# Expert tokens fetched by indirect DMA and transposed, instead of gathered by one-hot matmuls, in a trunk layer on one Trainium2 core

## The chip, the cores and the metric

The kernel runs on one core of a Trainium2 chip. The metric is the device time of one execution in microseconds. Engines: PE (TensorE: matmuls; PEld its weight loads), DVE (VectorE), ACT (ScalarE), POOL (GpSimd), SP (SyncE, which issues nearly all DMAs here).

## The reference, cut to what matters

A hybrid decoder layer on 512 tokens of 1024 features: a token mixer (RWKV-7 and sparse attention), a layer norm, then a mixture of 32 SwiGLU experts (top-1 of 4 groups, top-2 of 8 experts inside it), and a second layer norm. Everything is float32. The change is in the second half:

```
D_MODEL, SEQ, N_EXPERTS, TOP_K_INNER, D_EXPERT = 1024, 512, 32, 2, 512

def _hier_moe(x, wg, bg, we, be, w1, w3, w2):
    g_prob = jax.nn.softmax((xf @ wg + bg), axis=-1)
    grp = jnp.argmax(g_prob, axis=-1)
    ...
    top_v, top_i = lax.top_k(e_logits, TOP_K_INNER)      # inside the group
    top_w = jax.nn.softmax(top_v, axis=-1) * p_grp[:, None]
    ...
    xs = xpad[row_tok].reshape(n_blk, MOE_BLOCK, D)      # tokens of each expert
    def expert_block(args):
        xb, e = args
        h = jax.nn.silu(xb @ w1[e]) * (xb @ w3[e])
        return h @ w2[e]
    ys = lax.map(expert_block, (xs, blk_exp)).reshape(n_rows, D)
    out = jnp.zeros((N + 1, D), f32).at[row_tok].add(ys * row_w[:, None])

x = _layer_norm(ALPHA * x + token_mixer(x), ln1_g, ln1_b)
x = _layer_norm(ALPHA * x + _hier_moe(x, ...), ln2_g, ln2_b)
```

## The kernel before, in words

Up to about 560 us the mixer runs; then comes the output projection of its last columns with the first layer norm and the router (to 606 us), and then the experts. Instructions are recorded engine by engine and a tile framework orders them and sets the waits; each engine works in its own order.

**Router stage.** For each of four tiles t of 128 tokens, `normed(t)` writes the normalized x (without gain and bias) to x1 and, feature-strided, as a high and a low part into x1h (tile mh) and x1l (tile ml). `router` and `place` give each token its two experts and its slot there (posm); each expert has 64 slots, and tokens beyond these go to a loop `overflow` at the end, which runs as often as the counts ask (here not at all).

**Expert stage.** Sixteen pairs i of two experts. For each pair: W1 for both experts side by side (64 columns of slots each), then W3, into banks "a" and "o"; h = silu(W1 part) x (W3 part) on ACT and DVE (line 1674); four PE transposes of h; `slot_weights` (the routing weight of each slot, wv) and `slot_places` (the one-hot ST that brings slots back to tokens); W2 in two halves into banks "r" and "u"; and `scatter`, which multiplies ST with the result in two parts (yh, yl) and adds it on DVE to the sums. `scatter(0)` follows W2 of its pair, `scatter(1)` stands in the next pair. PSUM has three "w" banks, which all small matmuls share in turn.

**Gather.** For every four experts `places` makes the one-hot matrix G (DVE) and `gather` multiplies x1h and x1l with it: 8 x 4 x 2 matmuls of 128x256, whose results ACT and DVE write with the gain and the bias of the first norm to xe. The first gather (experts 0 to 3) is in the router stage; the others stand in pairs 1, 3, 5, 7, 9, 11 and 12.

**Weights.** 96 tiles of 2 MB (`order`: W1, W3, W2 of each pair) are loaded by SP in this order into a ring of tiles. Seven are loaded early, while the mixer still runs; later ones go into a tile as soon as its last reader is done. The first half of a tile may be filled while the second is in use (`half`, `begun`). Here x1 serves as a ring tile too once the first gather has read it, so the sums start anew in another tile ("k3") with `add_first`, and the residual (ALPHA times normalized x, from x1h + x1l) is added in pairs 4 and 5 by `residual`. In pair 12 two ring tiles are lent to xe2 and G. The last loads (`prefetch_pair`) are cut into small pieces.

**Tail.** After pair 15 and the loop `overflow`, the last quarter of the columns is scattered and the second layer norm is done, for which rows of ln2_g and ln2_b were broadcast by PE (`row`) in pairs 13 and 14.

Of the kernel before, what the change touches and what calls it, by code (L numbers as in the profile page):

```python
# [9 lines left out]
F32 = mybir.dt.float32  # L10
# [35 lines left out]
def _const_layout():  # L46
    lay, off = {}, 0
    for n, w in (("ident", 128), ("iota64", 64), ("rev32", 32), ("slot", 4), ("ones64", 128), ("ones2", 2), ("ma", 64),
                 ("mr", 64), ("lvl", 2 * 64), ("m16", 64), ("eye16", 256), ("rowm", 4), ("t5", 640), ("tri", 128)):
        lay[n] = (off, w)  # L50
        off += w
    return lay, off
# [6 lines left out]
def _consts():  # L59
# [30 lines left out]
    put("slot", np.broadcast_to((p % 64 + 1)[:, None], (128, 4)))  # L90
    put("tri", (p[:, None] < p[None, :]).astype(np.float32))
# [62 lines left out]
def trunk_kernel(ctx, tc, I, cst, out, dbg_outs=None, stop=None):  # L154
# [838 lines left out]
    def pools_up():  # L993
# [3 lines left out]
        mp = ctx.enter_context(tc.tile_pool(name="mp", bufs=1, side="right"))  # L997
# [159 lines left out]
    def first_half():  # L1157
# [4 lines left out]
        begun.append(into(units[order[0]], todo.index(order[EARLY + 2])))  # L1162
# [61 lines left out]
    wsp = sm("wsp", NT, 32, 2, dt=F32R)  # L1224
# [92 lines left out]
    def weights(t):  # L1317
# [11 lines left out]
        V_.tensor_copy(wsp[:, t, :, 0], wse[:, t])  # L1329
        V_.tensor_sub(wsp[:, t, :, 1], wse[:, t], wsp[:, t, :, 0].bitcast(F32))  # L1330
# [12 lines left out]
    def normed(t):  # L1343
# [58 lines left out]
    def gather_mm(p, k, ts, e0, start=True, stop=True):  # L1402
        for t in ts:
            for n, xx in enumerate((x1h, x1l)):
                pe.matmul(p, of(xx, t)[:, k], G_[e0][:, t].rearrange("p e s -> p (e s)"), start=start and t + n == 0,
                          stop=stop and t + n == NT, skip_group_check=not (start and stop))

# [4 lines left out]
    def gather_first(t):  # L1412
        for k in range(KD):
            gather_mm(pk[k], k, [t], 0, k % 2 == 0, k % 2 == 1)
# [21 lines left out]
    xe = me.tile([128, KD, 4, 64], F32, name="xe", tag="xe")  # L1436
    ia = [evacuate(xe, k, pk[k]) for k in range(KD)][-2]
# [47 lines left out]
    def gather(e0, xe=None):  # L1485
        places(e0, range(NT))
        xe = me.tile([128, KD, 4, 64], F32, name="xe", tag="xe") if xe is None else xe
# [4 lines left out]
        return xe  # L1492

    def slot_weights(e0):

        G, o = G_[e0 - e0 % 4], e0 % 4
# [4 lines left out]
        wv = me.tile([128, 2], F32, name="wv", tag="wv", bufs=2)  # L1501
# [4 lines left out]
        return wv[:, 0:1]  # L1506
# [32 lines left out]
    def residual(n):  # L1539

        g, b = row(0, n), row(1, n)
        for t in range(NT):
            r = me.tile([128, 512], F32, name="res", tag="res")
            h, l = (of(x, t)[:, :, 64 * n:64 * n + 64].bitcast(F32) for x in (x1h, x1l))
# [261 lines left out]
```

## Time and profile before

| | |
|---|---|
| median of 3 runs | 1153.6 us (1152.98 to 1154.99) |
| the profiled execution, its own time | 1153.26 us |
| its span, first to last instruction | 1151.4 us |
| PE busy | 1096.1 us, 95% |
| DVE, ACT, POOL busy | 47%, 29%, 23% |
| moved by DMA | 254.37 MB, of which 201 MB are expert weights |

The page cuts the span into 40 slices of 28.8 us. A digit is the busy share of a slice in tenths, PEclk the granted TensorE clock in tenths, DMA the busy share of the 16 DMA engines.

### The profile page before, as it was taken

How to read it: one execution, taken by the hardware profiler on the slowest of the kernel's cores; microseconds unless marked ns; L12 is line 12 of the kernel's file. 1: busy time of each engine (PE TensorE's matmuls, PEld its weight loads, DVE VectorE, ACT ScalarE, POOL GpSimd, SP SyncE). 2: the span in 40 equal slices, each digit the busy share in tenths (PEclk: the TensorE clock that was granted, in tenths of full speed). 3: DMA queues.
4: the chain of work that ended last, by engine and by line, in shares of the span. 5: the costliest groups of instructions: out<-in, count | busy, mean ns of one | idle time of the engine just before them, and what ended most of it. 6: DMA issues, size and time to landing. Idle time of an engine off the chain costs nothing. (4 is left out here: it accounts for less than half of the span.)

```text
span 1151.4 us, 16854 instructions
## 1 busy us (share of the span) xinstructions
PE 1096.1 (95%) x6526; PEld 686.7 (60%) x6526; DVE 536.7 (47%) x1320; ACT 338.4 (29%) x617; POOL 260.6 (23%) x251
## 2 busy tenths in 40 slices
PE   7999988999999999999979999999999999999992
PEld 5777766776766777888974444445353534454431
DVE  3673477478567643235494233255433323232225
ACT  5433434354462544424343111101010101111103
POOL 4442354264354335423040000010000000000002
PEclk9999899999999999999989999999999999999996
DMA  8561212211212201798547999898989999849931
GB/s 248 166 162 50 58 42 64 56 47 50 67 41 57 72 31 53 238 347 249 201 146 291 393 355 376 341 415 335 407 344 407 416 379 427 348 180 400 378 124 75
DMA packets 132626, 254.37 MB, mean 221 GB/s; under 512 B 31769, under 2 KB 88707, under 8 KB 126273
## 3 DMA queue, kind: packets, MB, share of 16 engines
q1 hardware_dynamic: 130816, 251.43, 60.1%
q0 software_dynamic: 1584, 1.78, 0.7%
q8 instruction: 53, 0.87, 0.3%
q14 instruction: 29, 0.23, 0.1%
q10 hardware_dynamic: 144, 0.07, 0.0%
HBM read 246.13 MB, written 7.62 MB: 220 GB/s over the span
## 5 line engine op out<-in xcount | busy, mean ns | idle before, releaser
L117 PE MATMUL ps_w<-xh,ws 128*128 128x512 f32 (+1 forms) x432 | 146.8, 422 | 3.0 <-ACT xh L258 1.9
L117 PE MATMUL ps_a<-wu,xe 128*64 128x512 f32 x600 | 138.4, 594 | 0.0
L117 PEld LDWEIGHTS ps_a<-wu,xe 128*64 128x64 f32 x600 | 43.8, 137 | 83.2 <-issue 82.0
L1524 DVE TENSOR_TENSOR xs<-xs,ps_w 128x512 f32<-128x512 f32 x112 | 71.9, 683 | 43.9 <-PE ps_w L117 43.0
L117 PEld LDWEIGHTS ps_w<-xh,ws 128*128 128x128 f32 (+1 forms) x432 | 77.0, 190 | 22.5 <-ACT xh L258 2.1
L117 PE MATMUL ps_w<-xl,ws 128*128 128x512 f32 (+1 forms) x216 | 86.6, 406 | 0.0
L239 POOL TENSOR_TENSOR ws<-wraw,ws 128x1024 fp32r<-128x1024 f32 (+2 forms) x31 | 66.8, 2153 | 75.6 <-ACT ws L238 75.5
L117 PE MATMUL ps_r<-wu,hT 128*64 128x512 f32 (+1 forms) x264 | 81.0, 618 | 0.7 <-ACT hT L1685 0.7
L1755 POOL TENSOR_TENSOR wu<-wu 128x512 f32<-128x512 f32 x1 | 2.1, 2142 | 329.0 <-ACT wu L1753 329.0
L117 PE MATMUL ps_w<-xh,w 128*128 128x512 f32 x224 | 75.8, 415 | 0.0
L117 PE MATMUL ps_u<-wu,hT 128*64 128x512 f32 (+1 forms) x248 | 68.0, 580 | 0.0
L117 PE MATMUL ps_o<-wu,xe 128*64 128x512 f32 x256 | 64.8, 594 | 0.0
L117 PE MATMUL ps_w<-yh,ST 128*128 128x512 f32 (+1 forms) x132 | 58.3, 453 | 6.0 <-issue 4.4
L1674 DVE TENSOR_TENSOR h<-h,ps_a 128x512 f32<-128x512 f32 x11 | 7.6, 689 | 118.8 <-PE ps_a L117 118.8
L883 POOL TENSOR_SCALAR pt<-pt,sm,gs 128x128 f32<-128x128 f32 (+3 forms) x64 | 44.9, 707 | 68.4 <-DVE sm L881 45.6
L1545 POOL TENSOR_TENSOR res<-mh,ml 128x512 f32<-128x512 f32 x8 | 10.4, 1296 | 202.9 <-DVE xs L1548 200.4
L117 PE MATMUL ps_w<-G,mh 128*128 128x256 f32 x216 | 54.1, 293 | 0.4 <-DVE ST L1636 0.4
L117 PE MATMUL ps_w<-G,ml 128*128 128x256 f32 x216 | 53.1, 288 | 0.0
L238 ACT CAST ws<-wraw 128x1024 fp32r<-128x1024 f32 (+2 forms) x43 | 39.6, 922 | 45.7 <-DMA wraw<-in_w_out_dram 16.5
L117 PEld LDWEIGHTS ps_w<-yh,ST 128*128 128x128 f32 x132 | 24.6, 191 | 47.7 <-issue 28.0
L880 ACT ACTIVATE pt<-pt,sm 128x128 f32<-128x128 f32 (+3 forms) x64 | 35.5, 556 | 57.7 <-DVE sm L878 57.1
L117 PE MATMUL ps_w<-yl,ST 128*128 128x512 f32 (+1 forms) x132 | 50.8, 396 | 0.0
(484 smaller groups left out, 2125.2 us busy)
## 6 DMA issues: line engine op xcount, KB each, us to landing
wu<-in_exp_w_dram SPq DMA_DIRECT2D x190, 512.0 KB, 10.2
wu<-in_exp_w_dram SPq DMA_DIRECT2D x32, 2048.0 KB, 11.6
wu<-in_exp_w_dram SPq DMA_DIRECT2D x24, 1024.0 KB, 8.5
wraw<-in_w_in_dram SPq DMA_DIRECT2D x36, 512.0 KB, 3.8
x<-in_exp_w_dram SPq DMA_DIRECT2D x12, 512.0 KB, 5.9
wraw<-in_w_out_dram SPq DMA_DIRECT2D x8, 512.0 KB, 4.9
rrep<-rrow_d SPq DMA_DIRECT2D x4, 640.0 KB, 8.8
xin<-in_x_dram SPq DMA_DIRECT2D x4, 512.0 KB, 6.1
```

The source lines that it names most:

```text
L117: return self.e.matmul(out, lhsT, rhs, **kw)
L238: hi_eng(hi[:, :w], raw[:, :w])
L239: (eng or nc.gpsimd).tensor_sub(lo[:, :w], raw[:, :w], hi[:, :w].bitcast(F32))
L880: nc.scalar.activation(pt[:, :n], pt[:, :n], AF.Exp, scale=-1.0, bias=sm[:, 0:1], accum_out=sm[:, 1:2])
L883: nc.gpsimd.tensor_scalar(pt[:, :n], pt[:, :n], sm[:, 1:2], gs[:, i, gi:gi + 1], op0=ALU.mult, op1=ALU.mult)
L1524: V_.tensor_add(x1[:, t, cols[n]], x1[:, t, cols[n]], p)
L1545: nc.gpsimd.tensor_add(r.rearrange("p (q k) -> p k q", k=KD), h, l)
L1674: V_.tensor_mul(h, h, fmajor(hs[1]))
L1755: last[eng] = fn(*a, **k)
```

## The change

- The tokens of experts 0 to 3 are gathered as before, into two tiles xe of 128 slots (one for each pair). For pairs 2 to 15 `gather` goes. `normed` writes x1 to a DRAM tensor xn_d. `pair(i)`, which takes the place of `slot_weights`, multiplies G with two more columns (the token numbers), so its result holds each slot's token number + 1; `row_indices` turns that into row numbers (empty slots get a number out of bounds, which the DMA skips), and `gather_rows` clears a tile xg on POOL and issues an indirect DMA that brings 128 rows of 4 KB. One pair later `turn` transposes xg on PE, 8 times 128x128, and ACT and DVE write xe.
- x1 keeps the sums from the start: the residual is applied in place, in pair 0, by two DVE operations for each tile. `add_first`, the tile res and the tile "k3" for the sums go.
- mh and ml join the ring of weight tiles, "k3" stays in it, x1 doesn't join: ten tiles. No tile is lent in pair 12.
- The rows of ln2_g and ln2_b come by a broadcasting DMA at the end of pair 14.
- The overflow loop fetches its tokens the same way; its work tile is a ring tile. The framework's DMA scratch is set to 2048.

```
@@ normed(t): after x1, x1h, x1l are written
-        if not t:
-            zt["kx"] = into(x1)
-        if t < NT - 1:
-            quarter(zt["kx"], t)
+        nc.sync.dma_start(xn_d[128 * t:128 * t + 128], x1[:, t])
...
-    slots += [(zt["xp"], "x1"), (wp, "wu")]
-    slots[:] = slots[EARLY + 1:] + slots[:EARLY + 1]
-    prefetch(1)
-    quarter(zt["kx"], NT - 1)
+    slots[:0] = [(wp, "wu"), (zt["mp"], "mh"), (zt["mp"], "ml")]
...
+    def xtile():
+        return me.tile([128, KD, 128], F32, name="xe", tag="xe", bufs=3)
+    xes = {0: xtile(), 1: xtile()}
+    for a in range(2):
+        ia = [evacuate(xes[a], k, pk[k][:, 128 * a:128 * a + 128]) for k in range(KD)][-2]
+    prefetch(3)
...
-    def gather(e0, xe=None):
-        places(e0, range(NT))
...
-        for k in range(KD):
-            p = bk("w")[:, 0:256]
-            gather_mm(p, k, range(NT), e0)
-            evacuate(xe, k, p)
+    def row_indices(v, n):
+        f, idx = (me.tile([128, 1], d, name="ix%d" % j, tag="ix%d" % j, bufs=2) for j, d in enumerate((F32, I32)))
+        V_.tensor_scalar(f[0:n], v, 0.0, 4096.0, op0=ALU.is_equal, op1=ALU.mult)
+        V_.scalar_tensor_tensor(idx[0:n], v, -1.0, f[0:n], op0=ALU.add, op1=ALU.add)
+        return idx
+    def gather_rows(v, n):
+        idx = row_indices(v, n)
+        xg = me.tile([128, D], F32, name="xg", tag="xg", bufs=2)
+        nc.gpsimd.memset(xg[0:n], 0.0)
+        nc.gpsimd.indirect_dma_start(out=xg[0:n], out_offset=None, in_=xn_d,
+                                     in_offset=bass.IndirectOffsetOnAxis(ap=idx[0:n, 0:1], axis=0),
+                                     bounds_check=S - 1, oob_is_err=False)
+        return xg
+    def pair(i):
+        G, o = G_[4 * (i // 2)], 2 * (i % 2)
         p = bk("w")
         for t in range(NT):
-            pe.matmul(p[:, 0:4], G[:, t, o:o + 2, :].rearrange("p e s -> p (e s)"),
-                      wsp[:, t, e0:e0 + 2, :].rearrange("p e x -> p (e x)"), start=t == 0, stop=t == NT - 1)
+            pe.matmul(p[:, 0:6], G[:, t, o:o + 2, :].rearrange("p e s -> p (e s)"), wsp[:, t, i], start=t == 0,
+                      stop=t == NT - 1)
...
+        if i > 1:
+            xgs[i] = gather_rows(p[:, 4:5], 128)
+    def turn(xg, xe, n=128):
+        for h in range(2):
+            p = bk("w")
+            for k in range(4):
+                pe.transpose(p[:, 128 * k:128 * k + n], xg[0:n, 4 * h + k::KD], ident[:n, :n])
+            for k in range(4):
+                evacuate(xe, 4 * h + k, p[:, 128 * k:128 * k + n])
@@ residual(n): g and b are broadcast by PE into two "w" banks, then for each t
-            nc.gpsimd.tensor_add(r.rearrange("p (q k) -> p k q", k=KD), h, l)
-            V_.tensor_mul(r, r, g)
-            V_.scalar_tensor_tensor(xs, r, ALPHA, xs, op0=ALU.mult, op1=ALU.add)
+            V_.scalar_tensor_tensor(xs, xs, ALPHA, g, op0=ALU.mult, op1=ALU.mult)
             V_.scalar_tensor_tensor(xs, b, ALPHA, xs, op0=ALU.mult, op1=ALU.add)
@@ for i in range(16)
-            if i == 12 and n:
-                xe2, G_[28] = unit([128, 2, KD, 4, 64]), unit([128, NT, 4, 64], F32R)
...
         elif not i:
+            residual(0)
             lists()
-            wv, ST = slot_weights(2 * i), slot_places(es)
+            pair(0)
+            pair(1)
+            wv, ST = wvs.pop(i), slot_places(es)
...
-        if i in (13, 14):
-            for n in range(2):
-                nc.scalar.copy(lnq[:, i - 13, 512 * n:512 * n + 512], row(i - 13, n))
         if not i:
             over = overflow_lists()
-        if i in (3, 5, 7, 9, 11):
-            xe = gather(2 * i + 2)
+            residual(1)
+        elif i < 15:
+            xes[i + 1] = xtile()
+            turn(xgs.pop(i + 1), xes[i + 1])
+        if i % 2 == 0 and i < 14:
+            places(2 * i + 4, range(NT))
+            pair(i + 2)
+            pair(i + 3)
...
+        if i == 14:
+            lnq = unit([128, 2, D])
+            for n, v in enumerate(("ln2_g", "ln2_b")):
+                nc.sync.dma_start(lnq[:, n], I[v][0:1].to_broadcast([128, D]))
```

Where instructions stand, first on PE in the second half of pair 1, from the slot weights to the end of W2 (wsp: the weights by slot; idb and posT: for ST; hT: transposed h; mh, ml: x in two parts; xg: the fetched rows). Before:

```order
L117 MATMUL ps_w<-wsp,G 128x4 x4
L117 MATMUL ps_r<-wu,hT 64x512
L117 LDWEIGHTS idb
L117 MATMUL ps_w<-posT,idb 64x512
L117 LDWEIGHTS idb
L117 MATMUL ps_w<-posT,idb 64x512
L117 MATMUL ps_r<-wu,hT 64x512 x7
L117 MATMUL ps_u<-wu,hT 64x512 x8
L117 MATMUL ps_w<-G,mh 128x256
L117 MATMUL ps_w<-G,ml 128x256
```

After:

```order
L118 LDWEIGHTS idb
L118 MATMUL ps_w<-posT,idb 64x512
L118 LDWEIGHTS idb
L118 MATMUL ps_w<-posT,idb 64x512
L118 MATMUL ps_r<-wu,hT 64x512
L122 MATMUL ps_w<-csm,xg 128x128 x8
L118 MATMUL ps_r<-wu,hT 64x512 x7
L118 MATMUL ps_u<-wu,hT 64x512 x8
```

The two rows that end the first piece are the start of 64 gathering matmuls; in their place stand the eight transposes, behind the first matmul of W2.

PE in pair 0, from the transposes of h on (gb: the rows of ln1_g and ln1_b that are broadcast; ps_o: W1 of pair 1). Before:

```order
L121 MATMUL ps_w<-csm,h 128x128 x4
L117 MATMUL ps_o<-x_4920,xe 64x512
L117 MATMUL ps_o<-wu,xe 64x512
L117 MATMUL ps_r<-wu,hT 64x512 x8
L117 MATMUL ps_u<-wu,hT 64x512 x8
```

After:

```order
L122 MATMUL ps_w<-csm,h 128x128 x4
L118 MATMUL ps_o<-wu,xe 64x512 x2
L118 MATMUL ps_w<-gb_5481,csm 128x128 x8
L118 MATMUL ps_w<-wsp,G 128x6 x4
L118 MATMUL ps_r<-wu,hT 64x512 x8
L118 MATMUL ps_u<-wu,hT 64x512 x3
L118 MATMUL ps_w<-wsp,G 128x6 x4
L118 MATMUL ps_u<-wu,hT 64x512 x5
```

The second broadcast of rows and the slot matmuls of pairs 2 and 3 now stand in W2 of pair 0; the first broadcast stands right behind W3 of pair 0.

ACT at the end of the program. Before:

```order
L1727 ACTIVATE yh<-ps_r,wv 128x256
L1730 ACT_TABLE_LOAD
L1730 ACTIVATE warm_5527<-yh,epsln 128x1
L1755 ACTIVATE sq,lsd<-xs,nmu 128x1024
L1753 ACTIVATE lsd<-lsd,epsln 128x1
```

After:

```order
L1750 ACT_TABLE_LOAD
L1750 ACTIVATE sq,lsd<-x_4920,nmu 128x1024
L1748 ACT_TABLE_LOAD
L1748 ACTIVATE lsd<-lsd,epsln 128x1
```

The last yh and its table load moved ahead of the overflow loop, and two table loads stand behind it.

## Rows read from the trace of the kernel before

**Rows 1.** The page: span, PE's busy share, and the slices (busy tenths of PE, granted clock, DMA share).

```profile
span 1151.4 us, 16854 instructions
PE 1096.1 (95%) x6526; PEld 686.7 (60%) x6526; DVE 536.7 (47%) x1320; ACT 338.4 (29%) x617; POOL 260.6 (23%) x251
...
PE   7999988999999999999979999999999999999992
...
PEclk9999899999999999999989999999999999999996
DMA  8561212211212201798547999898989999849931
```

**Rows 2.** Windows: start and end in us, length, busy us of each engine with its instructions, granted clock, DMA share, GB/s. First the whole expert stage to the last h, then three periods without a gather, one with a gather, the one in which two ring tiles were lent, and the last two.

```profile
605.80:1111.80 506.00, 504.16 (x2421) 228.08 (x2420) 173.00 (x367) 66.45 (x118) 9.04 (x7) 0.99 0.90 359
815.40:843.10 27.70, 27.65 (x123) 10.68 (x123) 8.41 (x16) 2.56 (x4) 0.00 (x0) 1.00 1.01 410
878.80:906.60 27.80, 27.76 (x123) 10.73 (x123) 8.47 (x17) 2.56 (x4) 0.00 (x0) 1.00 1.02 416
942.40:970.10 27.70, 27.66 (x123) 10.65 (x123) 8.41 (x17) 2.56 (x4) 0.00 (x0) 1.00 1.01 429
843.10:878.80 35.70, 35.67 (x187) 18.24 (x187) 11.96 (x24) 4.82 (x8) 0.00 (x0) 1.00 0.89 355
1006.50:1042.30 35.80, 35.75 (x187) 18.25 (x187) 11.95 (x24) 4.82 (x8) 0.00 (x0) 1.00 0.58 225
1042.30:1073.70 31.40, 31.37 (x139) 12.93 (x139) 8.43 (x16) 3.73 (x6) 0.00 (x0) 0.95 1.01 398
1073.70:1111.80 38.10, 37.15 (x152) 14.74 (x151) 12.48 (x25) 3.73 (x6) 0.00 (x0) 0.96 0.78 288
```

**Rows 3.** Timeline of DVE, the multiplication for h alone (start us, us; in brackets the idle time before it and its releaser): pairs 0, 1, 6, 7, 8, 13, 14 and 15.

```profile
619.85 0.69 DVE L1674 TENSOR_TENSOR h<-h,ps_a 128x512 f32<-128x512 f32 x1 [7.97 <-PE ps_a L117]
645.78 0.69 DVE L1674 TENSOR_TENSOR h<-h,ps_a 128x512 f32<-128x512 f32 x1 [11.07 <-PE ps_a L117]
...
815.37 0.69 DVE L1674 TENSOR_TENSOR h<-h,ps_a 128x512 f32<-128x512 f32 x1 [3.98 <-PE ps_a L117]
843.10 0.69 DVE L1674 TENSOR_TENSOR h<-h,ps_a 128x512 f32<-128x512 f32 x1 [12.36 <-PE ps_a L117]
878.82 0.69 DVE L1674 TENSOR_TENSOR h<-h,ps_o 128x512 f32<-128x512 f32 x1 [12.36 <-PE ps_o L117]
...
1042.33 0.69 DVE L1674 TENSOR_TENSOR h<-h,ps_a 128x512 f32<-128x512 f32 x1 [12.36 <-PE ps_a L117]
1073.71 0.69 DVE L1674 TENSOR_TENSOR h<-h,ps_o 128x512 f32<-128x512 f32 x1 [12.36 <-PE ps_o L117]
1111.84 0.69 DVE L1674 TENSOR_TENSOR h<-h,ps_a 128x512 f32<-128x512 f32 x1 [9.36 <-PE ps_a L117]
```

**Rows 4.** The instructions on tile G between 843 and 880 us: the gathering matmuls of pair 7 (duration ns least/median/most, first and last start).

```profile
L117 PE MATMUL ps_w<-G,mh x32: 279/281/386, 848.5 to 856.1; 128*128 128x256 f32 x32
L117 PE MATMUL ps_w<-G,ml x32: 279/281/285, 848.8 to 856.2; 128*128 128x256 f32 x32
```

**Rows 5.** Timeline of PE in pair 7: the four transposes of h and the matmul behind them.

```profile
843.93 0.60 PE L121 MATMUL ps_w<-csm,h 128*128 128x128 f32 x4
844.44 0.50 PE L117 MATMUL ps_w<-yh,ST 128*128 128x512 f32 x1
```

**Rows 6.** Timeline of PE: thirteen records of W2 in pair 1, then in pair 13 the broadcast of two rows and the thirteen records of W2 behind it.

```profile
649.86 3.22 PE L117 MATMUL ps_r<-wu,hT 128*64 128x512 f32 x13
...
1046.76 2.05 PE L117 MATMUL ps_w<-gb,csm 16*128 16x128 f32 x16
1048.73 4.91 PE L117 MATMUL ps_r<-wu,hT 128*64 128x512 f32 x13
```

**Rows 7.** First a group of DVE by line (count, busy us, mean ns): the residual's operation on 128x512; then the timeline of PE behind W3 of pair 0.

```profile
L1548 DVE SCALAR_TENSOR_TENSOR xs<-res,xs 128x512 f32<-128x512 f32 x8 | 5.5, 691 | 0.3
...
619.66 0.61 PE L121 MATMUL ps_w<-csm,posm 128*32 128x128 f32 x4
...
620.73 1.07 PE L117 MATMUL ps_o<-wu,xe 128*64 128x512 f32 x2
```

**Rows 8.** SP's own waits from 600 to 1110 us (us in total, times, longest), then DMA issues (count, KB each, median us to landing).

```profile
SPq L1106 <- PE ps_u L117: 105.0, 23, 18.7
SPq L1110 <- DMA wu<-in_exp_w_dram: 78.2, 72, 4.5
...
wu<-in_exp_w_dram SPq DMA_DIRECT2D x190, 512.0 KB, 10.2
wu<-in_exp_w_dram SPq DMA_DIRECT2D x32, 2048.0 KB, 11.6
...
qh<-ql POOLq DMA_DIRECT2D x8, 128.0 KB, 3.0
```

**Rows 9.** Timelines of the tail: PE's last matmuls of W2, then ACT.

```profile
1126.44 1.08 PE L117 MATMUL ps_r<-wu,hT 128*64 128x256 f32 x6
...
1129.00 1.28 ACT L1730 ACT_TABLE_LOAD   x1
...
1133.93 1.15 ACT L1755 ACTIVATE sq<-xs,nmu 128x1024 f32<-128x1024 f32 x1 [3.35 <-DVE nmu L1753]
...
1135.21 0.30 ACT L1753 ACTIVATE lsd<-lsd,epsln 128x1 f32<-128x1 f32 x1
```

**Rows 10.** A group of POOL: the memset of 128x256.

```profile
L822 POOL MEMSET Sc<- 128x256 f32 x4 | 1.3, 324 | 0.1
```

More of the change, by code (lines that the diff above doesn't have):

```diff
@@ L47, in _const_layout @@
     lay, off = {}, 0
-    for n, w in (("ident", 128), ("iota64", 64), ("rev32", 32), ("slot", 4), ("ones64", 128), ("ones2", 2), ("ma", 64),
+    for n, w in (("ident", 128), ("iota64", 64), ("rev32", 32), ("slot", 4), ("tok", 4), ("ones64", 128), ("ones2", 2), ("ma", 64),
                  ("mr", 64), ("lvl", 2 * 64), ("m16", 64), ("eye16", 256), ("rowm", 4), ("t5", 640), ("tri", 128)):
@@ L996, in pools_up @@
         mix.close()
-        mp = ctx.enter_context(tc.tile_pool(name="mp", bufs=1, side="right"))
+        mp = zt["mp"] = ctx.enter_context(tc.tile_pool(name="mp", bufs=1, side="right"))
         zt["mh"] = mp.tile([128, KD, S], F32R, name="mh")
@@ L1161, in first_half @@
         nc.sync.dma_start(half, usrc(*order[0])[:, 4:])
[L1162 removed]
+        begun.append(into(units[order[0]], todo.index(order[EARLY + 3])))
         for q in (2, 3):
@@ L1400, in trunk_kernel @@
     me = ctx.enter_context(tc.tile_pool(name="me", bufs=1, side="right"))
[L1402 to L1406, printed above, removed]
     places(0, range(NT - 1))
@@ L1413, in gather_first @@
         for k in range(KD):
-            gather_mm(pk[k], k, [t], 0, k % 2 == 0, k % 2 == 1)
+            for n, xx in enumerate((x1h, x1l)):
+                pe.matmul(pk[k], of(xx, t)[:, k], G_[0][:, t].rearrange("p e s -> p (e s)"), start=k % 2 == 0 and t + n == 0,
+                          stop=k % 2 == 1 and t + n == NT, skip_group_check=True)
     iv = place(NT - 1)
@@ L1575, in overflow @@
                                  ioc[:, None, :].to_broadcast([128, NT, 64]), op=ALU.is_equal)
-            Gw = pers.tile([128, NT, 64], F32R, name="Gw", tag="G")
+            Gw = pers.tile([128, NT, 64], F32, name="Gw", tag="G")
             V_.tensor_add(Gw, Gs[:, 0], Gs[:, 1])
+            p = bk("w")
+            for t in range(NT):
+                pe.matmul(p[0:64, 0:1], Gw[:, t], C("tok")[:, t:t + 1], start=t == 0, stop=t == NT - 1)
             xe = sl[:, 0:512].rearrange("p (k s) -> p k s", k=KD)
-            for k in range(KD):
-                p = bk("w")
-                n = 0
-                for t in range(NT):
-                    for xx in (x1h, x1l):
-                        pe.matmul(p[:, 0:64], of(xx, t)[:, k], Gw[:, t], start=n == 0, stop=n == 2 * NT - 1)
-                        n += 1
-                evacuate(xe, k, p[:, 0:64])
+            turn(gather_rows(p[0:64, 0:1], 64), xe, 64)
             hs = []
@@ L1652, in trunk_kernel @@
                     wk = zt["half"][:, k - 4] if i + n + a == 0 and k > 3 else w[a][:, k]
-                    m3 = pe.matmul(p[64 * a:64 * a + 64], xe[:, k, o + a, :], wk, start=k == 0, stop=k == KD - 1)
+                    m3 = pe.matmul(p[64 * a:64 * a + 64], xe[:, k, 64 * a:64 * a + 64], wk, start=k == 0, stop=k == KD - 1)
             hs.append(p)
@@ L1712, in trunk_kernel @@
                         mm = pe.matmul(p[64 * a:64 * a + 64], hT[:, f, 64 * a:64 * a + 64], w[a][:, f, cs], start=f == 0, stop=f == 3)
-            if n and not i:
-                slots.remove((zt["keep2"], "k3"))
-                x1 = zt["keep2"].tile([128, NT, D], F32, name="xs", tag="k3")
-            if n and i == 1:
-                xe = gather(2 * i + 2)
             if last and end:
@@ L1721, in trunk_kernel @@
             elif n and not end:
-                scatter(0, None if i else add_first)
-                if i in (4, 5):
-                    residual(i - 4)
+                scatter(0)
             yh = mh.tile([128, 512], F32R, name="yh", tag="yh")
```

68 lines of the change are left out of this document (25 added, 43 removed).

## The prediction, made before the changed kernel was run

> **What bounds the kernel now.** I read the page's shares and slices first. TensorE (PE) is busy 95% of the span, at 9 tenths or more in nearly every slice of the second half, with the granted clock at 1.0 there, while the DMA engines are also at 8 or 9 tenths in most of those slices [rows 1]. So two things are close to their limits from 600 us on, and the question is which of them waits for the other. The windows answer it: from the first expert matmul (605.8 us) to the last pair's gating (1111.8 us) PE is busy 504.2 of 506.0 us, and DMA runs at 0.90 of its engines, 359 GB/s [rows 2]. PE is the bound. DMA is not far behind: a pair without a gather takes 27.7 us, in which DMA share is 1.01 or 1.02 and 410 to 429 GB/s are moved [rows 2]. Those are saturated stretches. In pairs with a gather (35.7 us) the share falls to 0.89, because for 8 us no weight tile comes free [rows 2]. SP's own waits agree: 105 us of them are for PE to release a tile, 78 us for an earlier load to land [rows 8].
>
> The pace of the pairs is read from one instruction that every pair has once, the multiplication of the gate with the linear branch (h, line 1674), which I call the pair's mark. The first mark is at 619.85, the last at 1111.84: 492.0 us for 15 periods [rows 3]. A plain period (815.37 to 843.10) is 27.7, one with a gather (843.10 to 878.82) is 35.7 [rows 3]. The 64 gathering matmuls fill 848.5 to 856.2 us of the latter [rows 4], which is 7.7 us, and about 0.3 us is waiting around them. Fifteen plain periods would be 415.5; the remaining 76.5 us are seven gathers (7 x 8.0 = 56), two residual stages (about 6, pairs 4 and 5), and the last two periods, 31.4 and 38.1 us [rows 3], which hold row broadcasts, two clock dips and a wait for weights.
>
> **The change, part by part.** *Gathers.* Seven gathers go; each was PE work on the path: -56 us. *Turns.* In their place 14 pairs (2 to 15) get eight 128x128 transposes each. Four such transposes with h take 0.51 us from start to the next matmul [rows 5], so eight cost 1.0 us. They read x with a stride of eight and wait for PSUM banks that ScalarE and VectorE empty; neither is in the trace. From below it is 1.0, from above 2.5 us (the same again for the stride and 0.5 for a bank, the size of the waits around a gather). I take 1.3, nearer to the h transposes since they use the same banks and evacuations of the same kind: 14 x 1.3 = +18 us. The small matmuls for slot weights stay in number.
>
> *Rows and the residual.* The residual stages move from pairs 4 and 5 to pair 0, and the last layer norm's rows come by DMA, where PE broadcast them in pairs 13 and 14. Sixteen records of such a broadcast take 2.05 us, and right behind one in pair 13 thirteen expert records took 4.91 us where they take 3.22 elsewhere [rows 6]: the granted clock of that period is 0.95 [rows 2], that is, it fell from 2.4 to 1.2 GHz for a moment, at a price of 1.7 us. So pairs 13 and 14 lose 2 x 3.7 = -7.4, pairs 4 and 5 lose -6. In pair 0 there appear the same two broadcasts (+4.1), and they hold two of the three "w" banks while VectorE does eight operations of 0.69 us [rows 7]. Queued behind these on VectorE are the copy of the counts, the slot weights and ST, and PE waits for a bank: in the first residual until the sixth of the eight is done, 620.5 + 4.1 = 624.7, where PE has own work until about 622.8 (broadcast 2.05, transposes 0.6, one pair 0.5, from 619.66 [rows 7]); in the second some 4 us more, as the overflow lists stand between its operations. Together +10 us; from below 4, from above 15 (both series of 5.5 us in full).
>
> *Ring.* Pairs 14 to 15 waited for weights: 38.1 - 27.7 - 3.7 = 6.7 us. Its cause is at 1006.5 to 1042.3, with DMA at 0.58 [rows 2]: two ring tiles had gone to xe2 and G. With ten tiles in the ring and none lent, this goes: -6.7.
>
> *Gather DMAs.* Fourteen issues on POOL, which has 9.0 us of work in these 506 [rows 2]. A memset of 128x256 took 0.32 us [rows 10], so 128x1024 is about 1.3, off the path. The rows are needed one period after their indices, some 28 us later; a load of 2 MB lands in 11.6, one issued on POOL in a quiet stretch in 3.0 [rows 8]. Covered; if the cover went, each late microsecond would count 14 times.
>
> *Tail.* After the loop ScalarE now loads two tables, before Square and before Sqrt; before, one load of 1.28 us lay under a wait [rows 9]. The second stands between Square and Sqrt, and VectorE's reciprocal waits for that: +1.3. Writing x to DRAM (2.1 MB) falls in the router stage, where DMA is half idle [rows 1]: 0.
>
> **Sum.** The first mark stays at 619.85. The first period becomes 25.9 + 10 = 35.9 [rows 3], fourteen follow at 27.7 + 1.3 = 29.0, so the last mark is at 619.85 + 35.9 + 406 = 1061.8. The tail was 1151.4 - 1111.8 = 39.6 [rows 1, 3]; with 1.3 it ends at 1102.7 us of span.
>
> **Do the weights keep up?** 96 tiles of 2.10 MB are 201.3 MB. By 606 us seven and a half tiles and wp's have landed, 17.8 MB. What is left, with some 900 gathered rows of 4 KB (3.7 MB), is 187.2 MB. The last W2 pieces are wanted at about 1069, so 463 us, or 404 GB/s. The saturated windows gave 410 to 429 [rows 2]; a period of 29.0 us with 12.84 MB asks 443, so the lead of some eight tiles at 606 is eaten nearly whole by the end. At 400 GB/s the last piece lands at 1074, at 385 at 1092; the end comes 25 us behind it (0.4 us of matmul, then 1151.4 - 1127.5 [rows 1, 9]). I add 3 us for this: 1105.7 of span. The profiled execution took 1153.26 for 1151.4, so 1.9 lie outside; and it stands 0.3 under the median of 1153.6, which I leave out. Forecast: **1108 us**.
>
> A rule speaks against this. The Trainium skill, "DMA: Bandwidth & Descriptors", section Bandwidth, says that for HBM to SBUF one core's share of HBM, about 358 GB/s, binds, and not the 435 of the fabric. By it 187.2 MB would take 523 us and the end would be 1129 + 25 + 1.9 = 1156. The trace does not agree as it stands: 410 to 429 GB/s in three stretches of 28 us [rows 2].
>
> **Rivals.** *B, weights become the bound* (chance 0.20): for it speaks that the mean over the whole stretch is 359 GB/s, that the last pairs load in small pieces (398 in the window from 1042.3), and that gathered rows join the same engines; against it the three saturated windows. At 385 GB/s 1092 + 25 + 1.9 = 1119; from 1112 to 1140. *B2, the 358 of the page* (0.03): 1156, no gain. A real rate of 361 would return exactly the time of before.
>
> *C, the clock falls in every pair* (0.10). Transposes from rows and indices now stand together in the second half of a pair, as the broadcasts did in pairs 13 and 14, behind which the clock fell [rows 6]. At 1.7 us a pair, 14 pairs cost 24: 1132. Against it: the h transposes in 14 pairs of before left the clock at 1.0. The Trainium skill, "TensorE: Matmul & The Clock Gate", Part 4, says that transposes don't count as PE-busy in the way matmuls do; by it this rival would be the likelier, and no row here tells how much of that a pair can hold.
>
> *D, rows come late* (0.05), the case on the other side: PE's queue is in order, so a turn that waits for its rows holds W2, the scatter and the next pair's W1. It costs what a gather takes beyond 28 us, 14 times; from (1153.6 - 1108) / 14 = 3.3 us, that is from 31 us a gather, the kernel is slower; at 35 us a gather it would be 1108 + 98 = 1206. What could do it: indices out of bounds and 128 descriptors made in software, not measured here, and 2 MB loads ahead of the rows. SP has about eight loads open (10.2 us to landing at 1.28 us each [rows 8]); eight whole tiles are 41 us at 410 GB/s, but only pairs 10 and 11 load so.
>
> *E, less in the way than I count* (0.07): turns at 1.0, pair 0 at +4, weights in time: 1108 - 4 - 6 - 3 = 1095, down to 1088.
>
> **From these to the numbers.** My forecast A has 0.55 (1098 to 1118). Left out of 1092 to 1130 are parts of B and C (0.08), B2, D and a little of E: under 0.2. What a measurement tells from no change here is about 0.2%. Faster: A, most of B, C, E, 0.92; same 0.02; slower (D, B2) 0.06.
>
> **What would show it.** Right: marks 29.0 us apart in pairs 2 to 14, the first two 34 to 40; eight transposes a pair at about 0.13 us; no wait of PE on xg; DMA at 1.0 of its engines in most windows, near 420 GB/s. B: PE idle before expert matmuls with a DMA as releaser, growing toward the end. C: granted clock under 0.97 in plain windows. D: PE waiting for xg with POOL's queue as releaser. The forecast is most easily wrong in what a saturated DMA really gives over 450 us, and in the price of pair 0.

## The result, and where the time went

The changed kernel takes 1122.0 us (median of four runs, 1120.6 to 1127.6), the kernel before 1153.3 in the same comparison: a ratio of 0.974 (95% interval 0.970 to 0.978). The forecast was 1108, so it is 14 us above it, inside the range. The profiled execution has a span of 1120.0 us, where the working gave 1105.7.

The page of the changed kernel: busy shares, and the slices of PE, granted clock and DMA, as in [rows 1].

```profile
span 1120.0 us, 16280 instructions
PE 1057.4 (94%) x6158; PEld 643.6 (57%) x6158; DVE 546.3 (49%) x1380; ACT 347.5 (31%) x641; POOL 278.3 (25%) x275
...
PE   7999998999999999998997999999999999999992
...
PEclk9998899999999999999998999999999999999996
DMA  8652202302211311489743979999999999999971
```

The DMA row is at 9 from slice 25 to slice 38, where before it went between 8 and 9, with one slice at 4. The marks are read as in [rows 3] (timeline of DVE, the product h alone, here pairs 0, 1, 2, 10, 11, 12, 13, 14 and 15):

```profile
631.51 0.69 DVE L1677 TENSOR_TENSOR h<-h,ps_a 128x512 f32<-128x512 f32 x1 [6.69 <-PE ps_a L118]
666.18 0.69 DVE L1677 TENSOR_TENSOR h<-h,ps_a 128x512 f32<-128x512 f32 x1 [6.78 <-PE ps_a L118]
694.70 0.69 DVE L1677 TENSOR_TENSOR h<-h,ps_o 128x512 f32<-128x512 f32 x1 [12.36 <-PE ps_o L118]
...
926.53 0.69 DVE L1677 TENSOR_TENSOR h<-h,ps_a 128x512 f32<-128x512 f32 x1 [12.36 <-PE ps_a L118]
956.01 0.69 DVE L1677 TENSOR_TENSOR h<-h,ps_o 128x512 f32<-128x512 f32 x1 [12.37 <-PE ps_o L118]
986.78 0.69 DVE L1677 TENSOR_TENSOR h<-h,ps_a 128x512 f32<-128x512 f32 x1 [14.66 <-PE ps_a L118]
1017.56 0.69 DVE L1677 TENSOR_TENSOR h<-h,ps_a 128x512 f32<-128x512 f32 x1 [13.58 <-PE ps_a L118]
1046.08 0.69 DVE L1677 TENSOR_TENSOR h<-h,ps_o 128x512 f32<-128x512 f32 x1 [12.36 <-PE ps_o L118]
1080.45 0.69 DVE L1677 TENSOR_TENSOR h<-h,ps_a 128x512 f32<-128x512 f32 x1 [9.77 <-PE ps_a L118]
```

Against the forecast these marks give four differences, which sum to the 14.3 us that the span is longer:

| stretch | forecast | measured | difference |
|---|---|---|---|
| up to the first mark | 619.85 | 631.5 | +11.7 |
| first period | 35.9 | 34.7 | -1.2 |
| the fourteen periods after it | 406 + 3 | 414.3 | +5.3 |
| tail behind the last mark | 40.9 | 39.5 | -1.4 |

The middle of the program is as forecast: from 666.18 to 956.01 ten periods took 289.8 us, 29.0 each, by turns 28.5 and 29.5 (the slot matmuls of two pairs stand together in every second one). So the gain of the gathers is there, and nearly all of the miss lies at two ends: before the experts begin, and in the last four periods. The windows of five periods and of the whole expert stage (columns as in [rows 2]):

```profile
617.40:1080.50 463.10, 459.51 (x2053) 181.08 (x2052) 181.12 (x428) 70.90 (x138) 25.55 (x26) 1.00 1.00 404
666.20:694.70 28.50, 28.43 (x127) 11.12 (x127) 9.45 (x17) 4.36 (x8) 0.95 (x1) 1.00 1.03 419
926.50:956.00 29.50, 29.50 (x135) 12.02 (x135) 12.44 (x32) 4.36 (x8) 2.94 (x3) 1.00 1.02 424
956.00:986.80 30.80, 29.49 (x127) 11.19 (x127) 9.47 (x17) 4.36 (x8) 0.95 (x1) 1.00 1.00 426
986.80:1017.60 30.80, 30.55 (x135) 12.15 (x135) 11.06 (x29) 4.36 (x8) 2.94 (x3) 1.00 1.01 407
1046.10:1080.50 34.40, 32.73 (x136) 12.23 (x135) 12.80 (x22) 4.37 (x8) 0.00 (x0) 1.00 0.95 367
```

Over 463 us DMA moved 404 GB/s, which is the rate that the working asked for, with its engines busy all the time. PE was busy 459.5 us of it. Both engines are at their limit together: the change has used up the distance between them.

**The first mark.** I matched each instruction that both kernels have and took the difference of its start. It is 2.3 us at 500 us, 10.8 at 545, 11.7 at the first mark. So 8.5 us arise between 505 and 545 us, in the merge stage, which the diff does not touch. There SP issues (timeline of SP, issues of x, of gates and of merge weights alone; first before, then after; x is the layer's input, zg a gate, wraw a merge weight before it is split into a high and a low part):

```profile
473.24 0.60 SPq L1069 DMA_DIRECT2D x<-in_x_dram  x1
...
508.19 0.38 SPq L236 DMA_DIRECT2D wraw<-in_w_up_rwkv_dram  x1
...
512.75 0.38 SPq L236 DMA_DIRECT2D wraw<-in_w_up_rwkv_dram  x1
...
513.95 0.33 SPq L1045 DMA_DIRECT2D zg<-zg_d  x1
515.65 0.38 SPq L236 DMA_DIRECT2D wraw<-in_w_up_rwkv_dram  x1
```

```profile
508.19 0.38 SPq L237 DMA_DIRECT2D wraw<-in_w_up_rwkv_dram  x1
509.77 0.38 SPq L1070 DMA_DIRECT2D x<-in_x_dram  x1
515.98 0.34 SPq L1046 DMA_DIRECT2D zg<-zg_d  x1
516.41 0.94 SPq L237 DMA_DIRECT2D wraw<-in_w_up_rwkv_dram  x2
```

The load of x stands 36 us later, and the next merge weights now stand behind a load of zg, which waits until VectorE has finished a merge block. These are SP's waits for it between 505 and 530 us (total, times, longest; before, then after):

```profile
SPq L1045 <- DVE ml L1041: 1.9, 4, 0.7
```

```profile
SPq L1046 <- DVE ml L1042: 12.4, 4, 5.8
```

A late block thus makes the next weights late. PE then waits for split weights (waits of PE, 505 to 545 us: us in total, times, longest), and the granted clock, 1.0 in that window before, is 0.91:

```profile
PE ps_w L118 <- ACT w L239: 1.9, 1, 1.9
PE ps_w L118 <- ACT ws L239: 1.5, 2, 1.2
PE ps_w L118 <- DVE ws L240: 0.9, 1, 0.9
PE ps_a L118 <- DVE ws L240: 0.6, 1, 0.6
```

The cause that I then suspected is one number in the diff's last line: the DMA scratch of 2048 bytes. In the memory maps of the two programs all pools on the left lie 14,336 bytes a partition lower after the change (the Trainium skill, "SBUF — State Buffer", section "SBUF size: 192, 224, or 256?", gives the DMA-descriptor scratch as 16 KiB, and 16,384 - 2,048 is 14,336: the maps agree). The pools on the right stay. So x1's pool (bytes 163,616 to 180,192), which lay over the rw pool alone, now also lies over the yn pool (166,720 to 187,200 now, 181,056 to 201,536 before), and x's load must wait until yn's last reader is done.

### The profile page after: what moved, and what is told of

The parts are those of the page before. It is cut to its first block, busy times and chain, and to the rows that moved or that the text cites. A ratio compares the mean times of both kernels' runs of the same rounds, so it can differ in the third digit from the quotient of the medians.

```text
span 1120.0 us, 16280 instructions
## 1 busy us (share of the span) xinstructions
PE 1057.4 (94%) x6158; PEld 643.6 (57%) x6158; DVE 546.3 (49%) x1380; ACT 347.5 (31%) x641; POOL 278.3 (25%) x275
## 5 line engine op out<-in xcount | busy, mean ns | idle before, releaser
L118 PE MATMUL ps_a<-wu,xe 128*64 128x512 f32 x696 | 158.6, 594 | 1.5 <-DMA wu<-in_exp_w_dram 1.5
L118 PEld LDWEIGHTS ps_a<-wu,xe 128*64 128x64 f32 x696 | 50.2, 137 | 98.9 <-issue 91.0
L1544 DVE TENSOR_TENSOR x<-x,ps_w 128x512 f32<-128x512 f32 x120 | 77.0, 683 | 44.4 <-PE ps_w L118 43.3
L1497 POOL MEMSET xg<- 128x1024 f32 x14 | 13.3, 955 | 300.8 <-PE ps_w L122 298.3
L118 PE MATMUL ps_r<-wu,hT 128*64 128x512 f32 (+1 forms) x272 | 78.7, 591 | 0.7 <-ACT hT L1691 0.7
L118 PE MATMUL ps_o<-wu,xe 128*64 128x512 f32 x320 | 73.6, 595 | 0.0
L1691 ACT COPY hT<-ps_w 128x512 f32<-128x512 f32 x16 | 9.4, 587 | 127.0 <-PE ps_w L122 127.0
L118 PEld LDWEIGHTS ps_o<-wu,xe 128*64 128x64 f32 x320 | 22.7, 137 | 43.4 <-issue 40.7
L118 PEld LDWEIGHTS ps_w<-xl,ws 128*128 128x128 f32 (+1 forms) x216 | 41.0, 190 | 10.8 <-issue 0.9
```

Source lines behind the costliest of these rows:

```text
L118: return self.e.matmul(out, lhsT, rhs, **kw)
L1497: nc.gpsimd.memset(xg[0:n], 0.0)
L1544: V_.tensor_add(x1[:, t, cols[n]], x1[:, t, cols[n]], p)
L1691: nc.scalar.copy(hT, p.rearrange("p (f s) -> p f s", f=4))
```

## The experiments

On the chips of the experiments (three, and the kernel before ran on each) the clock fell more often in the mixer stage, in some executions more than in others; the kernel before took 1158 to 1162 us there. So whole times are compared by ratio, and the rest by marks within a trace. Marks and periods are those of one profiled execution of each kernel.

**The scratch alone**, on the kernel before:

```
-    nc = _bacc.Bacc("TRN2", target_bir_lowering=False, num_devices=1)
+    nc = _bacc.Bacc("TRN2", target_bir_lowering=False, num_devices=1, dynamic_dma_scratch_size=2048)
```

> The kernel before with one number of the change alone: the DMA scratch of 2048 bytes a partition. The pools on the left of SBUF then lie 14,336 bytes lower, x1's tile lies over the yn tile, and x's load stands 19 rows later in SP's queue. Theory L (place in memory): x's load moves from 473 to about 509 us, loads of merge weights come later, PE waits twice around 520 and 531 and the clock falls there; the first expert mark comes at 628 to 631 instead of 620, and the time is 8 to 12 us longer, 1161 to 1165. Theory R (the new work of the router stage, that is the writing of x to DRAM and the new slot weights, delayed the first mark): none of that is in this kernel, so no difference, 1152 to 1155.

Measured: 1174.2 against 1162.1, a ratio of 1.012 (1.007 to 1.017), slower by 8 to 19 us. x's load is issued at 515.0. Matched with the trace of before, its instructions are 7.6 us late at 500 us (clock falls of the mixer) and 17.1 at 545: 9.6 us in the merge stage. PE's waits in that window are those of the changed kernel:

```profile
PE ps_w L117 <- ACT w L238: 2.9, 1, 2.9
PE ps_w L117 <- ACT ws L238: 1.5, 2, 1.2
PE ps_w L117 <- DVE ws L239: 0.9, 1, 0.9
```

Theory L holds, R falls: nothing of the new router work is in this kernel.

**The shift undone**, on the changed kernel:

```
+    mix.enter_context(tc.tile_pool(name="pad", bufs=1)).tile([128, 3584], F32, name="pad")
     rw = mix.enter_context(tc.tile_pool(name="rw", bufs=1))
```

> The changed kernel with an unused tile of 14,336 bytes a partition under the mixer's tiles, so that these lie where they lay before, and x's load stands where it stood. Theory L: x's load at about 473 us again, the first mark at 620 to 623, 1110 to 1114. Theory R: the first mark stays at 631, 1121 to 1123. A third, W+: the first mark comes 9 us earlier but the weights do not, since the loads are the limit near the end; then the last three periods grow and the time is 1116 to 1121.

> The kernel with the pad once more, beside the one with the later residual stages on the same chip: theory L as before, first mark 9 to 12 us ahead of that of the changed kernel, 1109 to 1114 where the kernel before takes 1153, a ratio of 0.962 to 0.966.

Measured in two comparisons: ratios to before of 0.963 (0.957 to 0.968) and 0.964 (0.956 to 0.972), against 0.974 for the change as it was (0.971 when it was run once more). x's load is again far ahead of the merge weights, at 482.4. The profiled executions had clock falls ahead of 400 us, which hide the gain in their first marks (631.2 and 634.2, where I had expected 620 to 623). The stretch itself shows it: matched with the changed kernel's trace, this one is 6.9 us late at 500 us and 0.9 early at 550, so 7.8 us are won back there, and PE's waits in the window are 0.7 us in all. The four other traces with the pad, taken for the experiments below, win 6.7 to 8.7 us back in the same stretch; the five other traces of the changed kernel and its variants without it differ from its first by -1.7 to +0.2 there. The weights come earlier with it: the last four periods are 30.7, 30.8, 28.5 and 34.4, as in the changed kernel, so W+ falls. The first mark's miss is thus the layout; the remaining 3 us of it (2.3 ahead of 500 us, 0.9 behind 545) are of the size by which executions differ.

**Fewer loads**: pair 8 computes with the weights of pair 7, and its own are not loaded.

```
-    order = [(n, 2 * i + a) for i in range(16) for n in range(3) for a in range(2)]
+    order = [(n, 2 * i + a) for i in range(16) if i != 8 for n in range(3) for a in range(2)]
...
+        ew = es if i != 8 else (14, 15)
...
-            w = [units.pop((n, e)) for e in es]
+            w = [(units.get if i == 7 else units.pop)((n, e)) for e in ew]
...
```

> The changed kernel without the weights of pair 8: that pair computes with the weights of pair 7, so 12.6 MB are not loaded (30 us at 415 GB/s). Theory V (the loads are the limit near the end): the waits go from the last three periods, 30.8, 30.8 and 34.4 become 28.5, 29.5 and about 31.5 (three of the last are scatter work that the last pair does ahead of its mark), and the time falls by 5 to 7 us, to about 1116. Theory P (pieces: the small loads of the last pairs come late whatever the volume): the last period stays at 34.4, and the time falls by 0 to 4 us.

Measured: 1117.2 us; the fourteen periods after the first took 410.7, the last four of them 28.5, 29.5, 28.5 and 34.4. The first two waits are gone (3.6 us), so these were the loads. The last period did not move, although DMA had little to do in it:

```profile
1041.50:1075.80 34.30, 32.69 (x136) 12.20 (x135) 12.73 (x21) 4.36 (x8) 0.00 (x0) 1.00 0.59 208
```

Neither theory had that right. V gave 31.5, and P had the number but not the reason: with a DMA share of 0.59, and no DMA among PE's waits from 950 us on, it is not late small loads. The period has nine more PE records than its neighbours (136 to 127): pair 14's second scatter stands ahead of the last mark, and PE waits 0.8 us for yh and 0.6 for x there. It is the program's own length.

**No turns**: the rows are fetched, but not transposed.

```
-            xes[i + 1] = xtile()
-            turn(xgs.pop(i + 1), xes[i + 1])
+            xes[i + 1] = xe
```

> The changed kernel without the eight transposes a pair and their evacuations: the rows are still gathered, but every pair computes with the tokens of pair 0 or 1. PE has 14 x 1.16 = 16.2 us less to do. Theory T (PE sets the pace): the periods fall to 27.3 and 28.3 and the time by 14 to 17 us, to about 1106. Theory V (the loads are the limit from about 690 us on): the gain is used up by waits for weights, the periods are 27.3 and 28.3 only until the lead is gone, and the time falls by 1 to 5 us, to 1117 to 1121.

Measured: 1123.3 us. The fourteen periods took 411.4, where 414.3 - 16.2 = 398.1 would have been left by the transposes' own time. They run at 27.1, 29.1, 26.4 and 28.4 at first, where they were 28.5 and 29.5 by turns, so a turn with its evacuations costs PE up to 1.6 us a pair and not 1.16. An estimate from this pace and the last period of 32.4 is that PE alone would take about 388. From pair 7 on PE waits for weights, with DMA at 1.02 throughout:

```profile
808.10:836.50 28.40, 28.37 (x127) 11.06 (x127) 10.89 (x29) 2.56 (x4) 4.08 (x4) 1.00 1.02 415
836.50:868.50 32.00, 29.04 (x119) 10.39 (x119) 7.78 (x13) 2.56 (x4) 0.00 (x0) 0.95 1.02 414
868.50:899.00 30.50, 29.34 (x127) 11.21 (x128) 10.86 (x28) 2.56 (x4) 4.07 (x4) 1.00 1.02 414
899.00:932.40 33.40, 30.33 (x119) 10.77 (x120) 7.84 (x13) 2.56 (x4) 0.00 (x0) 0.90 1.02 415
```

and in the waits of PE from 660 to 1083 us:

```profile
PE ps_a L118 <- DMA wu<-in_exp_w_dram: 7.6, 4, 3.0
PE ps_o L118 <- DMA wu<-in_exp_w_dram: 3.8, 2, 2.9
```

So of the transposes' 16 us 13 are lost, and by the estimate of 388 some 23 in all. Behind these waits the clock falls as well (0.95 and 0.90). Theory V holds for the periods; the whole time is above its 1117 to 1121, with the first mark 2.9 us later than in the changed kernel and a first period of 36.4.

**No turns and no rows**: the indirect DMAs are left out too (beside the cut above).

```
-        nc.gpsimd.indirect_dma_start(out=xg[0:n], out_offset=None, in_=xn_d, ...)
```

> The kernel without turns once more, and now the rows are not gathered either: the indirect DMAs are left out, some 900 rows of 4 KB, 3.7 MB. Compared with the kernel without turns, whose last fourteen periods took 411.4 us. Theory V (the loads are the limit): the rows' 3.7 MB are 9 us at 415 GB/s, and the fourteen periods take 401 to 404. If the rows cost more than their bytes (their descriptors, their shape), the periods come down toward what PE alone needs, 388 (seven of 26.4, six of 28.3, the last 33). If the rows slip in beside the weights, 409 to 412.

Measured: 399.9 us for the fourteen periods, 11.5 less; the first wait comes two pairs later, at 903 us. By bytes it should be 9. As the first period was 34.7 here and 36.4 in the kernel without turns, the weights had 1.7 us less of a start, and the rows cost the DMA engines 11.5 to 13 us, by one execution of each kernel. The whole time is 1123.7 all the same, since the first mark comes at 647.9, 13.5 us later than without the turns alone. Twelve memsets of xg, which had waited for tiles with earlier rows, now run on POOL in one go from 615.45 to 626.22 us, and an operation of VectorE on 128x32 in the router stage, which takes 0.5 us for another tile, took 13.63 us beside them, until 626.25. The periods can be compared even so: at the first mark DMA had moved 75.6 MB in both kernels.

**Eight tiles in the ring**:

```
...
-    slots[:0] = [(wp, "wu"), (zt["mp"], "mh"), (zt["mp"], "ml")]
+    slots[:0] = [(wp, "wu")]
...
-    prefetch(3)
+    prefetch(1)
```

> The changed kernel with eight tiles in the weights' ring: the two tiles freed by the gathers stay unused. Theory V: two tiles of 2.10 MB less are loaded ahead when the pairs begin; that lead of 10 us is missing at the end, the waits begin some five pairs earlier, and the fourteen periods after the first take 420 to 424 instead of 414.3; time 1127 to 1132. If the ring only covers the delay of a load (11 us) and PE sets the pace: 414 to 416, 1121 to 1124.

Measured: 420.9 us for the fourteen periods, 1131.8 in all. The waits begin in the period from 932 us, which is 33.1 where it was 29.5: one period earlier than with ten tiles, not five, but then each of four periods waits. The size is as V had it: the two freed tiles are worth 6.6 us, all of it at the end, where their lead is spent. One of the four periods (32.5 us, granted clock 0.95) has a fall of the clock in it, so that between 5 and 6.6 us are the loads'.

**The residual stages later in pair 0**, on the kernel with the pad:

```
-            residual(0)
             lists()
...
             over = overflow_lists()
-            residual(1)
+            residual(0)
...
+            if not i and not n:
+                residual(1)
```

> The kernel with the pad, and in pair 0 the two residual stages stand later: the first behind the transposes of h, the second between the halves of W2, where PE has matmuls that need no bank of those that the stages hold. The first period was 34.7 to 36.4. If the price of pair 0 lies in waiting for banks beside the two broadcasts (4.1 us of PE), it falls to 30 to 31.5, and the time by 3 to 4 us against the kernel with the pad, a ratio to before of 0.959. If the loads take it back (theory V), the first period falls but the last three grow by as much, and the ratio stays at 0.962 to 0.963. If PE was not waiting in pair 0 at all, the first period stays over 34.

Measured: a ratio of 0.965 (0.957 to 0.973), by whole times no better than the pad alone, though at that width they could not show 3 us. The first period is 37.0 us, since the clock fell twice in it, each time right behind a broadcast of two rows (timeline of PE; sixteen records of W2 take 3.65 at full clock):

```profile
632.72 2.05 PE L118 MATMUL ps_w<-gb,csm 16*128 16x128 f32 x16
634.70 0.61 PE L118 MATMUL ps_w<-wsp,G 128*128 128x6 f32 x4
635.23 5.35 PE L118 MATMUL ps_r<-wu,hT 128*64 128x512 f32 x16
...
643.77 2.24 PE L118 MATMUL ps_w<-gb,csm 16*128 16x128 f32 x16
645.94 3.61 PE L118 MATMUL ps_u<-wu,hT 128*64 128x512 f32 x6
```

Without these two falls (1.7 us each) it would be 33.6, not the 30 to 31.5 expected: PE had not stood idle for banks. It had filled the time with W1 of pair 1, which stands between in pieces (timeline of PE in pair 0 of the changed kernel):

```profile
631.31 2.05 PE L118 MATMUL ps_w<-gb,csm 16*128 16x128 f32 x16
633.29 0.61 PE L122 MATMUL ps_w<-csm,posm 128*32 128x128 f32 x4
633.83 1.07 PE L118 MATMUL ps_o<-wu,xe 128*64 128x512 f32 x2
634.84 0.26 PE L118 MATMUL ps_w<-selb,oneb 128*128 128x32 bf16 x4
635.03 2.80 PE L118 MATMUL ps_o<-wu,xe 128*64 128x512 f32 x12
```

These pieces take longer together than in one run (PE by line in the first period of the changed kernel: count, busy us, mean ns; the 32 records of W3 in bank a took 7.9):

```profile
L118 PE MATMUL ps_o<-wu,xe 128*64 128x512 f32 x32 | 10.1, 610 | 0.0
```

The periods behind the first tell something else. The fourteen took 410.9, where the pad alone took 414.3: the waits of 30.7 and 30.8 became 28.5 and 29.8. In the first period of this kernel DMA moved 354 GB/s, which is 13.1 MB:

```profile
628.40:665.40 37.00, 37.00 (x167) 15.49 (x166) 23.38 (x71) 3.14 (x5) 2.15 (x2) 0.91 0.90 354
```

With the pad alone it was 318 GB/s (the window is shown below), or 11.6 MB. The 1.5 MB between them are 3.6 us at 415 GB/s, about what the waits near the end lost. From the first to the last mark this execution took 448.0 us, 2.7 less than with the pad alone, with one fall of the clock more. Why the loads came sooner was not tried.

**No residual in pair 0, and its rows by DMA**, both on the kernel with the pad. The first leaves the two stages out; the second loads the rows of the first layer norm into the two tiles xg, which are free until pair 0's end:

```
     prefetch(3)
+    ln1 = [me.tile([128, D], F32, name="xg", tag="xg", bufs=2) for _ in range(2)]
+    for g, v in zip(ln1, ("ln1_g", "ln1_b")):
+        nc.sync.dma_start(g, I[v][0:1].to_broadcast([128, D]))
...
-        g, b = row(0, n), row(1, n)
+        g, b = (r[:, 512 * n:512 * n + 512] for r in ln1)
```

> The kernel with the pad, without the residual stages of pair 0 (x is neither scaled nor given its bias there): 32 broadcast matmuls and 16 VectorE operations are left out. Theory B (the broadcasts are the price of pair 0: 4.1 us of PE, a clock that falls behind them in some executions, and W1 of pair 1 cut into short pieces between them): the first period falls from 34.7 or 36.4 to 28 to 30, and the granted clock stays at 1.0 in it. If it is the four groups of slot matmuls that stand there now, it stays over 32. Theory V for the rest: PE gains 5 to 8 us on the loads, so the waits near the end grow by 2 to 5 us and the fourteen periods after the first take 416 to 420 instead of 414.3.

> The kernel with the pad, with the rows of the first layer norm loaded by two broadcast DMAs (1 MB) into the two tiles of the gathered rows, where PE broadcast them in pair 0. Theory B: the first period falls to 28 to 30. Theory V: the loads give back most of it, since 1 MB is 2.5 us more and PE runs ahead of the weights sooner: the fourteen periods after the first take 417 to 422, and the time from the first mark to the last is 446 to 451, as with the pad alone (450.7) or up to 4 us less. If the loads were not the limit: 443 or less.

> The changed kernel once more, for a comparison with the two others on one chip: 1121 where the kernel before takes 1153, a ratio of 0.972 to 0.976, first period 34.7 or, where the clock falls in it, 36.4, and 414.3 us for the fourteen after it.

Measured: first periods of 29.1 and 29.6 us at a clock of 1.0, so theory B holds: the broadcasts and what they bring with them (the falls of the clock and the pieces of W1) are 5 to 7 us of the first period's 34.7 or 36.4. Without the residual one execution took 1112.0. What followed was better than V had it: 413.2 and 414.5 us for the fourteen periods, not 416 to 422. The loads took nothing back, because they too came sooner. With the rows by DMA the first period moved 410 GB/s; with the pad alone, 318 (both windows are the first period):

```profile
636.00:665.60 29.60, 29.60 (x135) 11.12 (x134) 18.86 (x63) 3.13 (x5) 3.10 (x3) 1.00 1.02 410
```

```profile
631.20:667.60 36.40, 36.40 (x167) 15.47 (x168) 23.32 (x72) 3.13 (x5) 2.22 (x2) 0.95 0.81 318
```

The kernel with pad and rows by DMA has the lowest ratio of all: 1113.4 us where before took 1159.0 and the change as it was 1126.1 on the same chip; ratios of 0.959 (0.952 to 0.966) and 0.971 (0.966 to 0.976). Its interval and that of the pad alone (0.963 and 0.964) overlap, so that its lead over the pad alone rests on the marks: from first to last mark it takes 444.1 us, the changed kernel 450.9 in that comparison, the kernel with the pad 450.6 and 450.7.

## Why the prediction was right or wrong, point by point

- **The range: held, but by its width.** 1122 lies above the 1098 to 1118 of my forecast A, in the part that the range had for B and C. Neither brought it there: 8.5 of the 14 us are the layout, for which the sum had no term, and 5.4 are the last period. That the range covered them is luck.
- **Gathers -56, turns +18: right.** The plain stretch runs at 29.0 a pair. 112 transposes of the rows took 16.2 us from the first to the last mark, 1.16 a pair where I had taken 1.3; the stride of eight cost nothing that shows. By the kernel without turns a pair is up to 1.6 us shorter, so that the rest of a plain period is nearer to 27.4 than to 27.7: that the sum came out at 29.0 to a tenth has two small errors in it that cancel.
- **"The first mark stays at 619.85": wrong, +11.7 us.** This step failed. I followed the diff's operations through the engines and did not follow its one change to memory. Some 8.5 us of it are the shift of the left pools by the smaller scratch, shown alone (+9.6) and undone (-7.8). No line of the diff speaks of the new order of SP's queue in the merge stage, but it was to be read from the built program before any run; I compared orders only in the expert stage.
- **Pair 0, +10: right in size, wrong in its make-up.** The first period grew by 8.8 (34.7 against 25.9), and by 10.5 in executions in which the clock fell there. PE was never idle in it; it is 4.1 us of broadcasts, 1.8 of slot matmuls that four pairs now have in it (2.4 us for sixteen, 0.6 for four before), and the rest is mostly W1 of pair 1 in pieces (10.1 us, where 32 such records in one run take 7.9). The wait for banks, the step of my sum for this term, did not come: with the stages moved away from the banks the period was 33.6 without its clock falls, 1.1 less.
- **"Wait for weights 14 to 15, -6.7": wrong.** This term was mis-sized by nearly all of it. [rows 3] gave 38.1 for that period, and 38.1 less the 3.7 of the broadcast is 34.4, which is what it still takes, now with a turn of 1.2 in it and with DMA at 0.59 too; without the turn it was 32.4. At most 2 of the 6.7 us were a wait. I had called a remainder a wait without having a row that said so, and [rows 2] said otherwise: PE is busy 37.15 of the 38.10 us of that period. The two ring tiles lent out, and DMA's 0.58 in [rows 2], had cost little or nothing there.
- **Broadcasts and clock falls in pairs 13 and 14, -7.4: right.** The granted clock is 1.00 there. Period 13 to 14 fell from 31.4 to 28.5, which with the turn of 1.2 is 4.1.
- **Weights keep up, +3: right, 3.6 measured** (30.8 for 28.5 and 30.8 for 29.5), in the periods from 956 and 987 us and not at the last pieces. But the margin was thinner than this sounds. By the no-turns kernel the bound behind it is about 411 us, 3 us below what the change takes: rival B was not the outcome, and yet nearly any further saving on PE alone behind the first period would have met it.
- **The rule against the change (B2) failed.** The Trainium skill, "DMA: Bandwidth & Descriptors", section Bandwidth, lets 358 GB/s bind; measured were 404 over 463 us and 407 to 426 in the full windows shown. I had taken its sentence without the note in the same section, which gives that share to each core where both cores of an HBM domain (two cores share one) stream; here one core ran. The Trainium skill, "Perfetto Trace Analysis", section Roofline, says that one core alone can go beyond that share up to about 435 GB/s; the trace agrees with that one. (By the sum in the prediction the time of before would come at 359.5 GB/s, not at 361.)
- **Rival C: not in the turns.** The clock is 1.00 in the windows of all plain periods, with twelve transposes in each. The rule of the Trainium skill on transposes that I had cited shows no effect here. What the clock does fall behind are the broadcasts of 16 rows, as in [rows 6]: in pair 0 it fell in six of the nine traces that have them there, and in neither of the two kernels without them.
- **Rival D: no.** The gathered rows landed 6.7 to 15.1 us behind their issue (median 9.2), and PE never waited for them.
- **Rival E: no.** Pair 0 cost 8.8 and a turn 1.2 to 1.6, not 4 and 1.0.
- **Tail, +1.3: the table load came** (1.28 us between Square and Sqrt), but 39.5 us were 1.4 less than forecast: from the last mark to the last yh it is 15.7 us, before 16.7. Before, ScalarE was idle for 5.57 us ahead of that yh and was released by the overflow loop (line 1560 on VectorE's queue); now the yh stands ahead of the loop, and it is 4.62 us, released by PE. I had no term for that. The clock has no part in it: it is 1.00 up to the last yh in both.

## What to carry to other kernels

When a change alters the size of any reserved or pooled memory, compare the order of every queue over the whole program, and look up what each tile newly lies on: a tile's place is a dependency. Call a remainder a wait only where a row names the releaser. When two engines run close to their limits, work out what each alone would take (here 411 us by the weights, in the kernel without turns, and 411 by PE, in the one with fewer loads; together they took 414): a saving on PE is kept where DMA has room (5 to 7 us in the first period), and mostly lost where it has none (at least 13 of 16 us without the turns).

## What was not expected of the hardware

- DMA held 404 GB/s over 463 us with engines busy all that time, with 512 KB and 2 MB loads and gathered rows together.
- 3.7 MB of gathered rows of 4 KB cost 11.5 to 13 us of DMA time, against 9 by bytes, in one execution of each of two kernels.
- Right behind sixteen matmuls that use 16 of 128 rows the granted clock fell to 1.2 GHz in some executions and not in others (at 643.8 us with the pad, not at all in the first period of the changed kernel's first trace), at a price of 1.5 to 1.7 us each time.
- Beside twelve memsets of 128x1024 on POOL, one operation of VectorE on 128x32 took 13.63 us and ended with the last of them (kernel without turns and rows); what held it was not tried.
- From the second period on the plain periods repeat to 0.1 us between executions, while what lies ahead of 500 us differed by up to 12 us between executions of the changed kernel and its variants, through clock falls; so a gain of 1% is read from marks sooner than from whole times.
